# A two-layer hybrid encoder: how the low halves of its weights are made

## The chip, the cores and the metric

The kernel runs on one core of a Trainium2 chip. The metric is device time in microseconds (us); less is better. PE is TensorE (matrix multiply), ACT ScalarE, DVE VectorE, POOL GpSimd, and SP is SyncE, whose queue issues the DMAs (transfers between memories).

## The reference

Two layers of an encoder on 512 tokens of width 1024, each with three residual parts. The mixer runs four groups of attention heads side by side, gates and sums them. Then come cross-attention into 256 memory tokens and a squared-ReLU MLP of width 4096.

```python
for layer in range(DEPTH):                      # DEPTH = 2
    h = rms(x, g_mix[layer])
    (aq, ..., gate) = jnp.split(h @ w_in[layer], split_points, axis=-1)   # 1024 x 7584
    o_a = diff_attention(...)                   # 4 heads
    o_b = mla(...)                              # 8 heads, latent projections
    o_c = window_gqa(...)                       # 8 heads, window of 128
    o_d = axial_gqa(...)                        # 8 heads, rotary
    br = jnp.einsum('bsmc,mcd->bsmd', o, w_branch[layer])
    x = x + jnp.einsum('bsmd,bsmd->bsd', sigmoid(gate), br) @ w_out[layer]
    x = x + memory_xattn(rms(x, g_x[layer]), rms(mem, g_mem[layer]), ...)
    u = rms(x, g_mlp[layer]) @ w_up[layer]
    x = x + jnp.square(jax.nn.relu(u)) @ w_down[layer]
```

All inputs are float32. The large weights are read once per layer, from HBM.

## The kernel before, in words

Every product of two float32 matrices is made of three PE matmuls on float32r operands (`mm3`): each operand x is split into a high part hi (x rounded to float32r) and a low part lo = x - hi, and the sum hi·hi + hi·lo + lo·hi is accumulated. So each weight chunk needs a high and a low tile before PE can use it.

The weights are packed into 352 chunks of up to 128 x 1024 floats (512 KB). `wload` (line 292) handles one chunk: SP loads it into a raw tile `wst` (line 295), ACT casts it into the high tile `whi` (line 299), and POOL subtracts in four quarters, raw minus high, into the low tile `wlo` (line 302; in the profile it is the helper's line 167). There are two `wst` tiles, four `whi` and four `wlo` (line 121). A raw tile is free for its next load when its cast and its four subtractions are done; a high or low tile is free when PE has finished the matmuls that read it. `chain("w")` and `chain("wh")` keep loads and casts in the order of the program.

The work of one layer is in three stages. The mixer (0 to about 690 us in layer 0, 1205 to 1857 in layer 1) has twelve attention units; each unit's input projection takes four chunks, or one for the latent heads, and the gate and branch products (`gate_piece`, `branch_piece`) are put between attention steps as filling work, in the places that the string `FILL` gives. Then come the output projection and the cross-attention (690 to 862, 1857 to 2033), and the MLP (862 to 1205, 2033 to 2362): 32 chunks up and 32 down, one chunk per 24 matmuls of 512 columns, nothing else on PE. In the MLP each `up` piece also puts two ACT instructions (ReLU on the PSUM tile, then Square, lines 1121 and 1122), and every second one a low-part subtraction on POOL (line 1125).

POOL's other work is small: powers of -0.5 for the norms (`rpow`, lines 311 and 312, and similar ones), on 128 x 4 to 128 x 12 numbers. They stand in the same queue as the subtractions, and an engine takes its queue in order.

The order of instructions on each engine is set at build time by a scheduler that simulates the program; the kernel states only the program order and the chains.

Of the kernel before, what the change touches and what calls it, by code (L numbers as in the profile page):

```python
# [12 lines left out]
AF = mybir.ActivationFunctionType  # L13
ALU = mybir.AluOpType
# [79 lines left out]
def kernel(  # L94
# [18 lines left out]
    V, A, G, T, SY = nc.vector, nc.scalar, nc.gpsimd, nc.tensor, nc.sync  # L113
# [12 lines left out]
    def tl(tag, shape, dt=F32):  # L126
        cnt[0] += 1
        return sp.tile(shape, dt, tag=tag, name=f"{tag}{cnt[0]}", bufs=BUFS[tag])
# [26 lines left out]
    def f(ap):  # L155
        return ap.bitcast(F32)
# [9 lines left out]
    def sub_lo(dst, src, hi, eng=None):  # L166
        (eng or V).tensor_tensor(out=dst, in0=src, in1=f(hi), op=ALU.subtract)  # L167
# [16 lines left out]
    def chain(key, first, last=None):  # L184

        if key in tails:
            tc.add_manual_dep(first.ins, tails[key].name,
                              mybir.DependencyInfo(mybir.DependencyClass.NoSync, mybir.DependencyReason.DATA), reason=key)
        tails[key] = (last or first).ins
# [102 lines left out]
    def wload(key, tag="wst"):  # L292
        off, n = PLAN[key]
        st = tl(tag, [P, 1024])
        i = SY.dma_start(st[:, :n], bass.AP(tensor=wts.tensor, offset=wts.offset + off, ap=[[n, P], [1, n]]))
        chain("w", i)
        hi = tl("whi", [P, 1024], F32R)
        lo = tl("wlo", [P, 1024], F32R)
        chain("wh", A.copy(hi[:, :n], st[:, :n]))  # L299
        step = n // 4 if n % 4 == 0 else n // 2  # L300
        for c in range(0, n, step):
            sub_lo(lo[:, c:c + step], st[:, c:c + step], hi[:, c:c + step], G)
        return hi[:, :n], lo[:, :n]

    def wview(w, k):
# [124 lines left out]

    def front_A(l, norm, h):
        views = [wview(wload((l, "A", h, c)), k=2) for c in range(4)]
        vt = tl("v", [P, NTB, 2, P], F32R)
        Tq = tslot()
# [97 lines left out]

    def front_G(l, norm, br, g):
        views = [wview(wload((l, br, g, c)), k=2) for c in range(4)]
        vt = tl("v", [P, NTB, 3, 64], F32R)
        Tq = [tslot(), tslot()]
# [117 lines left out]

    def front_B0(l, norm, pre):
        views = [wview(w, k=2) for w in pre + [wload((l, "B", 0, c)) for c in range(len(pre), 4)]]
        cT = [slot(), slot(), slot()]
        toks = []
# [337 lines left out]
    for m in range(KD):  # L996
        SY.dma_start(X[m // 2][:, m % 2, :], xT[m * P:(m + 1) * P, :])
        if m % 2 == 0:
            c = m // 2
# [279 lines left out]
```

## Time and profile before

| | us |
|---|---|
| median of 3 runs | 2372.52 (2371.97 to 2377.07) |
| profiled execution, whole time | 2373.54 |
| its span, first to last instruction | 2371.8 |
| PE busy in the span | 2287.5 |
| POOL busy, all of it | 1304.7 |
| POOL busy with the weights' subtractions (1400 recorded) | 1079.1 |
| ACT busy with the weights' casts (350 recorded) | 349.9 |
| ACT busy, all of it | 1154.2 |

Between the span and the whole time lie 1.7 us. The granted clock of TensorE was 0.992 of full speed over the span. Matmuls overlap in the record: one of 512 columns shows 0.39 us, and the next starts 0.23 us after it. The busy share of an engine is a mean over stages; where the chain of waits names POOL or a DMA, PE was not the engine whose work ended last. Each wait is put down to one releaser, the one that came last.

### The profile page before, as it was taken

The numbers are of one execution on the slowest core, as the hardware profiler recorded it, in microseconds if no ns is written. First come the engines' busy times: TensorE is split into PE (matmuls) and PEld (weight loads), VectorE is DVE, ScalarE is ACT, GpSimd is POOL, SyncE is SP. The second block draws the span as 40 slices with busy tenths as digits, with TensorE's granted clock in tenths as the row PEclk, the third lists the DMA queues.
The fourth block names the chain that finished last, engine by engine and source line by source line (L and its number), as shares of the span: only waits on it lengthen the run. The fifth ranks groups of instructions, "written<-read, shape, count | busy, mean of one in ns | idle before, by whom it ended". The sixth has DMA issues, their size and how long they took to land.

```text
span 2371.8 us, 33721 instructions
## 1 busy us (share of the span) xinstructions
PE 2287.5 (96%) x12032; PEld 1963.8 (83%) x12032; DVE 1395.6 (59%) x2996; ACT 1154.2 (49%) x2269; POOL 1304.7 (55%) x1657
## 2 busy tenths in 40 slices
PE   7999999998999999999999999999999999999999
PEld 6788888887877788888888888898888778888887
DVE  6777676788964742222457676768888558322222
ACT  4555656655643642223345565566556446322321
POOL 7553454635365576666665435455453655766663
PEclk9999999999999999999999999999999999999999
DMA  5332242442454233333342213324425532323332
GB/s 169 103 96 68 89 138 76 138 145 80 151 170 151 76 98 96 91 98 98 107 132 92 87 56 106 133 78 150 131 88 168 169 107 85 103 94 98 98 93 85
DMA packets 90953, 260.36 MB, mean 110 GB/s; under 512 B 9832, under 2 KB 14568, under 8 KB 90784
## 3 DMA queue, kind: packets, MB, share of 16 engines
q1 hardware_dynamic: 90784, 258.20, 34.2%
q8 instruction: 95, 1.56, 0.3%
q14 instruction: 74, 0.61, 0.1%
HBM read 224.56 MB, written 33.60 MB: 109 GB/s over the span
## 4 chain that ended last, share of the span: by engine, by line
PE 73%; DVE 10%; POOL 7%; DMA 4%; ACT 3%; issue 3%; SPq 0%; POOLq 0%; ACTq 0%; DVEq 0%
PE dn L177 12%; PE dn L178 12%; PE dn L179 12%; PE df L177 9%; PE df L179 8%; PE df L178 8%; POOL wlo L167 5%; DMA wst<-in_wts_dram 3%; PE tr L476 2%; PE dn L403 1%; ACT whi L299 1%; DVE pt L480 1%; PE sc L177 1%; PE sc L178 1%; PE sc L179 1%
## 5 line engine op out<-in xcount | busy, mean ns | idle before, releaser
L167 POOL TENSOR_TENSOR wlo<-wst,whi 128x256 fp32r<-128x256 f32 (+3 forms) x1400 | 1079.1, 803 | 796.3 <-ACT whi L299 705.8
L299 ACT CAST whi<-wst 128x1024 fp32r<-128x1024 f32 (+3 forms) x350 | 349.9, 1002 | 663.3 <-PE dn L178 293.9
L177 PE MATMUL df<-s,whi 128*128 128x512 f32 (+1 forms) x967 | 383.2, 396 | 21.3 <-DVE zg L785 11.6
L178 PE MATMUL df<-s,whi 128*128 128x512 f32 (+1 forms) x967 | 376.7, 390 | 0.3 <-DVE s L167 0.3
L179 PE MATMUL df<-s,wlo 128*128 128x512 f32 (+1 forms) x967 | 376.8, 390 | 0.0
L177 PE MATMUL dn<-whi,s 128*128 128x384 f32 (+4 forms) x736 | 249.3, 345 | 12.0 <-ACT s L348 7.5
L178 PE MATMUL dn<-wlo,s 128*128 128x384 f32 (+4 forms) x736 | 250.0, 342 | 1.0 <-POOL wlo L167 1.0
L179 PE MATMUL dn<-whi,s 128*128 128x384 f32 (+4 forms) x736 | 250.1, 341 | 0.0
L177 PEld LDWEIGHTS df<-s,whi 128*128 128x128 f32 x967 | 182.8, 189 | 60.0 <-DVE zg L785 13.6
L179 PEld LDWEIGHTS df<-s,wlo 128*128 128x128 f32 x967 | 182.8, 189 | 37.1 <-POOL wlo L167 0.7
L178 PEld LDWEIGHTS df<-s,whi 128*128 128x128 f32 x967 | 182.9, 189 | 33.4 <-DVE s L167 0.8
L178 PE MATMUL dn<-s,whi 128*128 128x512 f32 (+1 forms) x529 | 198.8, 377 | 0.2 <-DVE s L167 0.2
L177 PE MATMUL dn<-s,whi 128*128 128x512 f32 (+1 forms) x529 | 198.0, 377 | 1.1 <-DVE s L976 0.9
L179 PE MATMUL dn<-s,wlo 128*128 128x512 f32 (+1 forms) x529 | 197.6, 374 | 0.0
L177 PEld LDWEIGHTS dn<-whi,s 128*128 128x128 f32 x736 | 140.1, 191 | 21.2 <-ACT s L348 7.5
L479 ACT CAST pt<-tr 128x512 fp32r<-128x512 f32 (+1 forms) x224 | 123.1, 557 | 68.6 <-PE tr L476 67.0
L480 DVE TENSOR_TENSOR pt<-tr,pt 128x512 fp32r<-128x512 f32 (+1 forms) x224 | 142.7, 643 | 20.0 <-ACT pt L479 9.5
L178 PEld LDWEIGHTS dn<-wlo,s 128*128 128x128 f32 x736 | 140.8, 191 | 11.0 <-POOL wlo L167 4.3
L179 PEld LDWEIGHTS dn<-whi,s 128*128 128x128 f32 x736 | 140.4, 191 | 5.3
L311 POOL TENSOR_SCALAR sf<-sf 128x8 f32<-128x8 f32 (+2 forms) x44 | 13.2, 299 | 193.7 <-DVE sf L415 192.0
L177 PEld LDWEIGHTS dn<-s,whi 128*128 128x128 f32 x529 | 99.7, 190 | 19.8 <-DVE s L976 1.1
L178 PEld LDWEIGHTS dn<-s,whi 128*128 128x128 f32 x529 | 100.4, 190 | 18.6 <-DVE s L167 0.6
(392 smaller groups left out, 4895.9 us busy)
## 6 DMA issues: line engine op xcount, KB each, us to landing
wst<-in_wts_dram SPq DMA_DIRECT2D x272, 512.0 KB, 3.6
wst<-in_wts_dram SPq DMA_DIRECT2D x64, 384.0 KB, 3.1
yl<-yz SPq DMA_DIRECT2D x48, 512.0 KB, 3.8
yz<-zg SPq DMA_DIRECT2D x64, 256.0 KB, 2.1
yz<-yl SPq DMA_DIRECT2D x48, 256.0 KB, 2.9
bias<-tscr SPq DMA_DIRECT2D x16, 320.0 KB, 3.5
yl<-yz SPq DMA_DIRECT2D x16, 256.0 KB, 3.1
bias<-tscr SPq DMA_DIRECT2D x8, 448.0 KB, 3.5
```

The lines of the kernel that those rows point to most:

```text
L167: (eng or V).tensor_tensor(out=dst, in0=src, in1=f(hi), op=ALU.subtract)
L177: a = T.matmul(ps, lhsT=lh, rhs=rh, start=first, stop=False)
L178: T.matmul(ps, lhsT=lh, rhs=rl, start=False, stop=False)
L179: b = T.matmul(ps, lhsT=ll, rhs=rh, start=False, stop=last)
L299: chain("wh", A.copy(hi[:, :n], st[:, :n]))
L311: G.tensor_scalar(dst, src, add, None, op0=ALU.add)
L403: T.transpose(ps[:rows_, i * P:(i + 1) * P], s, idn)
L476: T.transpose(ps[:, kb * P:(kb + 1) * P], src[:, kb * P:(kb + 1) * P], idn)
L479: A.copy(hi, pv)
L480: V.tensor_tensor(out=lo, in0=pv, in1=f(hi), op=ALU.subtract)
```

## The change

The four subtractions on POOL are replaced by two steps: ACT writes the negated high part into the low tile, and a DMA issued from POOL's queue adds the raw chunk onto it, element by element, in place.

```diff
         hi = tl("whi", [P, 1024], F32R)
         lo = tl("wlo", [P, 1024], F32R)
         chain("wh", A.copy(hi[:, :n], st[:, :n]))
-        step = n // 4 if n % 4 == 0 else n // 2
-        for c in range(0, n, step):
-            sub_lo(lo[:, c:c + step], st[:, c:c + step], hi[:, c:c + step], G)
+        A.activation(lo[:, :n], hi[:, :n], AF.Copy, scale=-1.0)
+        G.dma_start(out=f(lo[:, :n]), in_=st[:, :n], accum_op=ALU.add)
         return hi[:, :n], lo[:, :n]
```

Lines after 302 carry a number one less in the changed kernel. ACT gains one instruction per chunk. In the MLP of layer 0 its queue read before:

```order
922 L299 CAST whi_10667<-wst_10665 128x1024
923 L299 CAST whi_10704<-wst_10702 128x1024
924 L1121 ACTIVATE p_10582<-dn_10557 128x512
925 L1122 ACTIVATE p_10582<-p_10582 128x512
926 L299 CAST whi_10744<-wst_10742 128x1024
927 L299 CAST whi_10781<-wst_10779 128x1024
928 L1121 ACTIVATE p_10659<-df_10634 128x512
929 L1122 ACTIVATE p_10659<-p_10659 128x512
```

and at the same place it reads now (line 300 is the negation; `df` and `dn` are PSUM tiles that PE writes):

```order
1079 L299 CAST whi_10446<-wst_10444 128x1024
1080 L300 ACTIVATE wlo_10447<-whi_10446 128x1024
1081 L299 CAST whi_10481<-wst_10479 128x1024
1082 L1120 ACTIVATE p_10365<-df_10340 128x512
1083 L300 ACTIVATE wlo_10482<-whi_10481 128x1024
1084 L1121 ACTIVATE p_10365<-p_10365 128x512
1085 L299 CAST whi_10519<-wst_10517 128x1024
1086 L300 ACTIVATE wlo_10520<-whi_10519 128x1024
1087 L299 CAST whi_10554<-wst_10552 128x1024
```

The negation of every second chunk stands behind a ReLU that waits for PE.

POOL's queue in layer 0's mixer, at the second pair of powers of a projection (`sf` are norm sums), read before:

```order
81 L311 TENSOR_SCALAR sf_2720<-sf_2720 128x8
82 L312 TENSOR_TENSOR sf_2720<-sf_2720,mhalf 128x8
83 L167 TENSOR_TENSOR wlo_2883<-wst_2880,whi_2882 128x256 x4
84 L167 TENSOR_TENSOR wlo_3088<-wst_3085,whi_3087 128x256 x4
85 L311 TENSOR_SCALAR sf_2782<-sf_2782 128x8
86 L312 TENSOR_TENSOR sf_2782<-sf_2782,mhalf 128x8
87 L167 TENSOR_TENSOR wlo_3131<-wst_3128,whi_3130 128x192 x4
```

and now, with line 301 the accumulating DMA:

```order
79 L310 TENSOR_SCALAR sf_2658<-sf_2658 128x8
80 L311 TENSOR_TENSOR sf_2658<-sf_2658,mhalf 128x8
81 L301 DMA wlo_2821<-wst_2818 128x1024
82 L301 DMA wlo_3024<-wst_3021 128x1024
83 L310 TENSOR_SCALAR sf_2720<-sf_2720 128x8
84 L311 TENSOR_TENSOR sf_2720<-sf_2720,mhalf 128x8
85 L301 DMA wlo_3065<-wst_3062 128x768
```

The powers keep their places; between the two pairs stand two DMA issues where eight subtractions stood. The order of PE's instructions in both MLPs is the same in the two kernels (runs of 1506 and 1469 rows); in the mixers it differs in details.

## Rows read from the trace of the kernel before

**Rows 1.** The page's head, busy times, and shares of the chain that ended last.
```profile
span 2371.8 us, 33721 instructions
...
PE 2287.5 (96%) x12032; PEld 1963.8 (83%) x12032; DVE 1395.6 (59%) x2996; ACT 1154.2 (49%) x2269; POOL 1304.7 (55%) x1657
...
PE 73%; DVE 10%; POOL 7%; DMA 4%; ACT 3%; issue 3%; SPq 0%; POOLq 0%; ACTq 0%; DVEq 0%
```

**Rows 2.** Windows: stretch, us, busy us (instructions) by engine, clock, DMA, GB/s.
```profile
862.00:1205.00 343.00, 343.00 (x1502) 281.17 (x1501) 95.01 (x127) 107.21 (x136) 222.03 (x263) 1.00 0.34 101
690.00:862.00 172.00, 165.22 (x881) 138.06 (x880) 104.27 (x172) 85.58 (x163) 98.02 (x120) 0.99 0.39 119
0.00:690.00 690.00, 650.16 (x3693) 574.40 (x3694) 521.82 (x1232) 399.00 (x859) 352.11 (x473) 0.99 0.36 117
```

**Rows 3.** The chain of waits by line, 862 to 1205 us.
```profile
by line: PE dn L178 22.1%; PE dn L179 22.1%; PE dn L177 22.0%; PE df L177 11.2%; PE df L178 11.2%; PE df L179 11.2%; PE tr L364 0.2%
```

**Rows 4.** Timeline of ACT: start, us, engine, line, [idle before, releaser].
```profile
1002.38 1.05 ACT L299 CAST whi<-wst 128x1024 fp32r<-128x1024 f32 x1 [4.41 <-PE df L178]
1003.34 0.59 ACT L1121 ACTIVATE p<-df 128x512 f32<-128x512 f32 x1
1003.96 0.63 ACT L1122 ACTIVATE p<-p 128x512 f32<-128x512 f32 x1
...
1018.92 1.05 ACT L299 CAST whi<-wst 128x1024 fp32r<-128x1024 f32 x1 [3.33 <-PE df L178]
```

**Rows 5.** Timeline of POOL, same stretch.
```profile
1003.51 3.47 POOL L167 TENSOR_TENSOR wlo<-wst,whi 128x256 fp32r<-128x256 f32 x4 [2.30 <-ACT whi L299]
```

**Rows 6.** Waits of PE: releaser, us in total, times, longest.
```profile
PE dn L178 <- POOL wlo L167: 1.0, 3, 0.4
```

**Rows 7.** Chain of waits in time, 778 to 804 us: start, us.
```profile
782.07 3.54 DMA wst<-in_wts_dram
...
790.47 3.77 DMA wst<-in_wts_dram
...
795.44 3.92 POOL wlo L167 x4
...
799.38 3.62 DMA wst<-in_wts_dram
```

**Rows 8.** DMA issues: count, KB each, median us to landing.
```profile
wst<-in_wts_dram SPq DMA_DIRECT2D x272, 512.0 KB, 3.6
...
s<-in_xT_dram SPq DMA_DIRECT2D x8, 256.0 KB, 5.3
```

**Rows 9.** DMA queue, 862 to 1205 us: packets, MB, share.
```profile
q1 hardware_dynamic: 10160, 34.48, 33.3%
```

**Rows 10.** The chain of waits by line, the four stages outside the MLPs.
```profile
by line: PE df L177 8.6%; PE df L179 8.0%; PE df L178 8.0%; POOL wlo L167 6.7%; PE dn L177 5.8%; PE dn L178 5.7%; PE dn L179 5.5%; issue 4.9%; PE tr L476 4.0%; DMA wst<-in_wts_dram 3.7%; DVE zr L584 2.0%; DVE pt L480 2.0%; PE dn L403 1.8%; 
...
by line: POOL wlo L167 12.6%; PE dn L178 12.5%; PE dn L177 12.4%; PE dn L179 12.0%; DMA wst<-in_wts_dram 6.4%; PE df L177 5.0%; PE df L179 5.0%; PE df L178 5.0%; ACT whi L299 2.5%; PE sc L177 2.2%; PE sc L178 2.1%; PE sc L179 2.1%; PE tr L1
...
by line: PE df L177 8.2%; PE df L179 7.7%; PE df L178 7.7%; PE dn L177 6.4%; PE dn L179 6.3%; PE dn L178 6.2%; issue 4.8%; POOL wlo L167 4.7%; DMA wst<-in_wts_dram 4.1%; PE tr L476 3.4%; PE dn L403 2.2%; DVE pt L480 1.9%; ACT whi L299 1.7%;
...
by line: PE dn L177 13.6%; PE dn L178 13.6%; PE dn L179 13.2%; POOL wlo L167 9.1%; DMA wst<-in_wts_dram 8.2%; PE df L178 5.1%; PE df L179 4.8%; PE df L177 4.8%; ACT whi L299 2.3%; PE sc L177 2.3%; PE sc L178 2.2%; PE sc L179 2.2%; PE tr L17
```

**Rows 11.** Timeline of POOL in layer 0's mixer, around 288 us.
```profile
280.81 0.24 POOL L311 TENSOR_SCALAR sf<-sf 128x8 f32<-128x8 f32 x1 [5.22 <-DVE sf L415]
...
288.08 5.07 POOL L167 TENSOR_TENSOR wlo<-wst,whi 128x256 fp32r<-128x256 f32 x8 [5.27 <-ACT whi L299]
293.24 0.24 POOL L311 TENSOR_SCALAR sf<-sf 128x8 f32<-128x8 f32 x1
```

**Rows 12.** Timeline of DVE: one add beside POOL's subtractions, one without.
```profile
752.82 1.24 DVE L339 TENSOR_TENSOR of<-of,p 128x512 f32<-128x512 f32 x1
...
1915.41 0.68 DVE L339 TENSOR_TENSOR of<-of,p 128x512 f32<-128x512 f32 x1
```

**Rows 13.** Windows of line 299 alone: ACT busy us (casts).
```profile
0.00:690.00 690.00, 87.58 (x92) 0.99 0.36 117
```


## The prediction

> **What bounds the kernel now.** I read the page's head first: PE is busy 2287.5 of 2371.8 us, and the chain that ended last is 73% PE, 10% DVE, 7% POOL, 4% DMA, 3% ACT [rows 1]. Then the windows by stage: in the MLP PE is busy all of 343 us at full clock, in the mixer 650 of 690, in output projection and cross-attention 165 of 172 [rows 2]. So a gain can only come from outside the MLPs, and little of it.
>
> The MLP's chain of waits is PE alone [rows 3]. The reader is to see how the weights arrive there: ACT's casts come 5.51 us apart (1002.38 to 1018.92, three steps), each released by PE giving back a high tile [rows 4], and POOL's four subtractions end 3.47 us after they start, then POOL idles [rows 5]. That is a supply running four chunks ahead, held back by PE. PE waited for a low tile 1.0 us in the whole program [rows 6].
>
> In the other four stages the chain of waits contains the supply itself: POOL's `wlo`, the loads of `wst` and the casts, as far as the lines show them, are 10.4% of 690, 21.5% of 172, 10.5% of 652 and 19.6% of 176 us, together 212 us [rows 10]. In order of time it is a loop through one raw tile: load 3.54, cast 1.06, subtraction 3.4, load 3.77, cast, subtraction 3.92, load [rows 7]. The loads start 8.40 and 8.91 us apart, mean 8.66; about 0.25 of it is neither load (3.65), cast (1.06) nor subtraction (3.7).
>
> **The change, part by part.** *Removed*: 1400 subtractions on POOL. In the MLP they were hidden by PE, so there this is worth nothing. *Added on ACT*: one negation per chunk. ACT has no such row; the nearest is the cast of the same 128x1024 tile, 1.05 us [rows 4]; I take 1.06. ACT's queue in the MLP sets a ReLU (0.59 us) between cast and negation of every second chunk. *Added on POOL's queue*: one accumulating DMA per chunk, which waits for the negation; the raw tile is now free only when it has landed. *Moved*: nothing in PE's order in the MLPs.
>
> The price that decides is X, the time from the issue of the accumulating DMA to its landing. No transfer of this kind is in the trace. From below: a plain 512 KB load lands after 3.6 us [rows 8]; nothing suggests that reading, adding and writing back takes less. From above: the slowest landing in these rows, 5.3 us for 256 KB with many transfers in flight [rows 8], plus another 3.6 for the second operand, 8.9. In between: the 512 KB loads of the MLP keep 33.3% of the 16 DMA engines busy [rows 9], so one load costs 0.333 x 5.51 = 1.83 us of all of them; the second operand adds that once more, and as a third of the time a load is under way I add a third of it again, 0.6: 3.6 + 1.8 + 0.6 = 6.0. I take 6.0, nearer to the plain load than to the queue of the first microseconds.
>
> The loop through one raw tile then is 3.65 + 1.06 + 1.06 + 6.0 + 0.25 = 12.0 us instead of 8.66, and with two raw tiles one chunk comes per 6.0 us; in the MLP the ReLU makes it 12.6, one chunk per 6.3 us.
>
> - MLPs: PE wants a chunk every 5.51 us and gets one every 6.3. The four high tiles hide the first four of 128 chunks: 124 x 0.79 = +98 us. The cover goes where the loop passes 2 x 5.51 = 11.0, at X = 4.4.
> - Other stages, supply already on the chain: 212 x (12.0 / 8.66 - 1) = +82 us.
> - Other stages, supply not on the chain now: output projection and cross-attention take 24 chunks per layer, largely at the MLP's pace: 48 x (6.0 - 5.5) = +24 us. In the mixer 92 casts fall in 690 us, 7.5 us each [rows 2, 13], so the mean is covered, and I add nothing.
> - ACT: behind each negation stand the attention's exponentials and PSUM copies. ACT was 399 of 690 us busy in the mixer [rows 2], and 3% of the chain [rows 1]. Some 220 negations fall outside the MLPs; if one in fifteen delays the chain by its 1.06 us, +15 us; the bounds are 0 and, at one in four, 58.
> - POOL's queue: at 280.81 us a pair of powers runs, the next pair runs at 293.24, behind 5.07 us of subtractions [rows 11]. Now two DMA issues stand there, which wait for casts and negations. With an issue of some 1 us (bounds: 0, and the 2.5 us of one chunk's subtractions here) about 1.5 us is saved in each of some 16 such places, eight projections in halves per layer: -25 us.
> - DVE: an add of 128x512 takes 1.24 us beside the subtractions and 0.68 without [rows 12]. If an eighth of the chain's DVE time (10%, 237 us) is such stretching, -30 us. The two savings together I bound by -20 and -110.
>
> The Trainium skill's page SBUF — State Buffer, section "SBUF: two separate sides", agrees with the DVE row and adds what speaks against the change: a DMA of POOL's queue has its descriptors written by GpSimd, which is locked out while DVE runs an op in a two-port mode. No run here shows it yet; it would lengthen X where DVE is busiest, in the mixer.
>
> Sum: 98 + 82 + 24 + 15 - 25 - 30 = +164 us. Against the profiled execution's own 2373.5 (span 2371.8 and 1.7 around it) that gives 2538; this execution lies 1.0 above the median of the runs shown, so I forecast **2537 us**.
>
> **The rivals.**
>
> *1. The accumulating DMA lands like a plain load, and POOL's relief wins (faster).* With X = 3.6 the loop is 9.6 us: the MLPs lose nothing (10.2 / 2 = 5.1), the stages outside lose 212 x 0.11 = 23, ACT 15, and 55 is saved: -17, 2356 us. It decides as soon as the savings exceed 38 us. For it: 1079 us of POOL's work goes, and the waits of rows 11. Against it: PE waited for low tiles 1.0 us, and the new path has a step more. Here the Trainium skill's page DMA: Bandwidth & Descriptors, section "Anatomy of one DMA — SWDGE (gpsimd) path", gives a fit, 2.0 us plus bytes over 436e3; for 512 KB that is, as an estimate by that page, 3.2 us, and the sum by it 2346. The fit is one for copies, and the plain loads of this trace took 3.6, not 3.2.
>
> *2. Just covered.* X between 4.2 and 5: at 4.4 the loop is 10.4, the MLP exactly even, the rest +43 + 15 - 55 = +3, 2376 us; at 5, MLP +36, rest +57 + 15 - 55, 2426.
>
> *3. The DMA engines or their adder become the bound.* If the accumulate costs the engines three passes (two reads and a write, one after the other), a chunk takes 1.83 + 3 x 1.83 = 7.3 us of all 16, more than PE's 5.51; a long X comes to the same. At X = 8 the loop gives MLP 7.3 per chunk, +222, outside +131 and +72, ACT and savings -40: 2758. At 8.9: +278, +153, +94, -40, 2858. For it: engines already a third busy; against: nothing yet, the operation is not in the trace.
>
> *4. The change doesn't take load off POOL*, if generating a DMA holds it as long as the subtractions did, 3.5 us. Then savings vanish and X grows by that time; it ends in rival 3.
>
> **How the numbers follow.** Forecast, X from 5 to 8: 0.45, own range 2426 to 2758. Rival 2, X from 4.4 to 5: 0.13, slower by up to 53 us. Rival 3 with 4: 0.24. X under 4.4: 0.18, of which 0.14 is rival 1 (faster) and 0.04 ends within 0.2%, which is about 5 us and what a measurement of this kernel can tell from no change; I add 0.01 to that from rival 2. So faster 0.14, same 0.05, slower 0.81. The range goes from 2356 (X at its lower bound; half of rival 1 lies below) to 2870 (just past the upper bound, some 0.12 beyond): 0.81 inside.
>
> **What would show it.** In the changed profile: in the MLP windows PE no longer busy all the time, and the casts released by the loads instead of PE; their distance is the loop over two, 6.3 us expected. The chain of waits in the MLP should name the DMA `wlo<-wst`, and the DMA view its landing, 6.0. DMA share in the MLP from a third to about two thirds, near full in rival 3. L339-like DVE rows at 0.7 us everywhere would show the relief. Forecast wrong: casts still 5.5 us apart and released by PE (X under 4.4), or distances above 7.3.

## The result and the profile after

The changed kernel takes 2693.31 us (median of 4 runs, 2685.90 to 2716.57), the kernel before 2372.24 us beside it: a ratio of 1.1365, 95% interval 1.1291 to 1.1439. The forecast was 2537 us, slower by 6.9%; it went to 13.6%, inside the range of 2356 to 2870. The profiled execution took 2716.57 us, the longest of the four, with a span of 2714.8, 343.0 more than the span of before; the stages below add up to these 343, where the medians differ by 321. One run further below, 2738.82 us, lies more than 1.5% above the fastest of its kernel and enters no comparison.

The page's head, against [rows 1]:

```profile
span 2714.8 us, 33387 instructions
...
PE 2408.1 (89%) x12032; PEld 2011.8 (74%) x12032; DVE 1266.4 (47%) x2996; ACT 1460.9 (54%) x2621; POOL 532.4 (20%) x601
...
DMA 45%; PE 32%; issue 11%; ACT 8%; DVE 2%; POOL 1%; SPq 0%; POOLq 0%; ACTq 0%; DVEq 0%
DMA wlo<-wst 25%; DMA wst<-in_wts_dram 18%; PE dn L178 4%; PE dn L179 4%; PE df L177 4%; PE df L179 4%; PE dn L177 4%; PE df L178 4%; ACT wlo L300 3%; ACT whi L299 2%; PE tr L475 2%; PE sc L177 1%; PE sc L178 1%; PE sc L179 1%; DMA yl<-yz 1
```

The chain was 73% PE and 4% DMA; now it is 45% DMA, and 25% of the span is the accumulating DMA alone. POOL was relieved (1304.7 to 532.4 us busy), DVE too (1395.6 to 1266.4), and neither decides anything. PE works 120.6 us longer on the same 12032 matmuls, and the windows show why. They follow the stages of the changed kernel (stretch, us, busy us of PE, its weight loads, DVE, ACT, POOL, then clock, DMA share, GB/s), against [rows 2]:

```profile
0.00:833.00 833.00, 728.75 (x3893) 630.24 (x3894) 490.10 (x1262) 492.90 (x975) 172.62 (x204) 0.95 0.63 161
833.00:977.00 144.00, 120.17 (x655) 100.96 (x654) 66.89 (x136) 83.34 (x155) 21.16 (x27) 0.94 0.58 141
977.00:1391.00 414.00, 371.52 (x1504) 284.28 (x1503) 88.24 (x127) 169.07 (x205) 79.77 (x82) 0.98 0.72 164
```

In the MLP of layer 0 PE is idle 42 of 414 us where it was never idle, and the DMA share has gone from 0.34 to 0.72. In the mixer PE is idle 104 of 833 us, and its clock is 0.95 of full speed, so its work takes longer too; before, the mixer cut at the same place reads

```profile
0.00:735.00 735.00, 695.16 (x3890) 611.33 (x3891) 542.95 (x1261) 412.16 (x876) 375.38 (x501) 0.99 0.38 121
```

with 40 us idle. Two waits of PE and one of ACT in mixer 0 (releaser, us in total, times, longest):

```profile
PE dn L178 <- DMA wlo<-wst: 26.2, 11, 6.5
PE df L179 <- DMA wlo<-wst: 15.6, 10, 5.5
...
ACT whi L299 <- DMA wst<-in_wts_dram: 136.5, 40, 7.0
```

PE waits 41.8 us for low parts themselves, where it was 0.4 us before. ACT's casts wait 136.5 us for loads (41.1 before), and the attention's instructions stand behind them in ACT's queue.

Cut at the starts of the first addition of the output projection (line 1075 of before), of the MLP's first ReLU (line 1121) and of its last addition (line 1139), the profiled executions divide so:

| us | mixer 0 | projection, cross-attention 0 | MLP 0 | mixer 1 | projection, cross-attention 1 | MLP 1 |
|---|---|---|---|---|---|---|
| before | 735.1 | 116.3 | 345.3 | 710.2 | 115.3 | 345.5 |
| after | 832.9 | 143.7 | 414.5 | 789.5 | 138.7 | 391.7 |
| difference | +97.8 | +27.4 | +69.2 | +79.3 | +23.4 | +46.2 |

So the mixers pay 177 us, the MLPs 115 and the middle stages 51, together 343. (The middle stages are shorter here than in [rows 2], since part of their chunks is cut off to the mixer.)

The chain of waits in time, layer 0's MLP (start, us, what), answers [rows 3, 7]:

```profile
1198.45 4.36 DMA wst<-in_wts_dram
...
1202.89 0.04 ACT whi L299
...
1203.84 0.59 ACT p L1120
1204.43 0.95 ACT wlo L300
1205.39 0.28 issue
1205.67 6.91 DMA wlo<-wst
...
1212.63 4.55 DMA wst<-in_wts_dram
...
1220.05 6.22 DMA wlo<-wst
...
1226.32 4.13 DMA wst<-in_wts_dram
```

This is the forecast's loop, in its order: load, cast, ReLU, negation, accumulation, next load into the same raw tile. It runs 14.18 and 13.69 us, 6.97 per chunk with two raw tiles, where PE wants one every 5.51. (Over the whole stage it is less: 5.51 x 414.5 / 345.3 = 6.6 us per chunk, and 6.2 in layer 1.) The DMA view of 977 to 1391 us gives the price (queue, packets, MB, share of 16 engines; then issues, count, KB each, median us to landing), against [rows 8, 9]:

```profile
q0 software_dynamic: 9128, 33.12, 41.6%
q1 hardware_dynamic: 9912, 34.36, 30.6%
...
wlo<-wst POOLq DMA_DIRECT2D x62, 512.0 KB, 6.1
wst<-in_wts_dram SPq DMA_DIRECT2D x60, 512.0 KB, 4.2
```

X is 6.1 us here, 6.0 was taken. What the sum did not have is that the loads beside it became slower, from 3.6 to 4.2. In layer 1's MLP the two raw tiles fell into step for some 100 us, and the chain reads:

```profile
2401.17 5.24 DMA wlo<-wst
...
2406.47 3.73 DMA wst<-in_wts_dram
...
2412.71 4.42 DMA wlo<-wst
...
2417.18 4.61 DMA wst<-in_wts_dram
...
2424.31 4.45 DMA wlo<-wst
```

POOL now issues two accumulations 2.4 to 2.8 us apart, where it issued them some 7 us apart in the stretch above. So they run mostly beside each other, one lands after 4.4 to 5.2 us, and the loop is 11.54 and 11.60 us, 5.8 per chunk. It does not last. The issues of 2400 to 2500 us, and of 2500 to 2600:

```profile
wlo<-wst POOLq DMA_DIRECT2D x18, 512.0 KB, 4.8
...
wlo<-wst POOLq DMA_DIRECT2D x14, 512.0 KB, 6.3
```

PE is busy 99.7 of the first 100 us and 87.4 of the second. MLP 0 has both landings too: 6.7 us from 1060 to 1140, 4.8 from 1300 to 1373. So MLP 1's smaller loss (46 us against 69) fits more time in step, but no run holds the step fixed.

Two smaller answers, in the views by line (durations as minimum, median and maximum in ns). POOL's issue of the DMA in mixer 0, against [rows 5]:

```profile
L301 POOL DMA_DIRECT2D wlo<-wst x97: 850/863/1004, 7.7 to 832.4; - x97
```

And DVE's addition, now line 338, in 833 to 977 us, against [rows 12]:

```profile
L338 DVE TENSOR_TENSOR of<-of,p x21: 411/419/686, 841.5 to 965.1; 128x256 f32<-128x256 f32 x14, 128x512 f32<-128x512 f32 x7
```

An issue holds POOL 0.86 us instead of 3.47 for the subtractions (rival 4 wanted 3.5), and none of these additions takes 1.24 us any more.

Last, what such a wait leaves behind on PE. In mixer 0 the chain names an accumulation from 264.94 to 270.61 us and a load from 270.66 to 273.65; the windows around them:

```profile
265.00:268.00 3.00, 1.10 (x7) 0.71 (x6) 1.97 (x4) 2.06 (x6) 1.10 (x3) 1.00 1.04 205
...
274.00:277.00 3.00, 1.27 (x8) 0.68 (x7) 1.95 (x4) 2.95 (x7) 1.19 (x2) 1.00 0.63 122
...
278.00:281.50 3.50, 3.50 (x17) 2.75 (x15) 0.73 (x2) 0.65 (x2) 0.00 (x0) 0.57 1.03 216
281.50:285.00 3.50, 3.50 (x21) 3.22 (x20) 1.89 (x4) 2.73 (x5) 0.41 (x1) 1.00 0.78 261
```

PE works 1.10 of the first 3 us, is busy from 268 to 274, works 1.27 of the next 3 us and is busy again from 277; then the granted clock falls to 0.57 for 3.5 us (most of it at 1.2 instead of 2.4 GHz) before it is full again. So a wait can be paid twice: once idle, once at the lower clock.

### The profile page after: what moved, and what is told of

It is laid out like the page before. It is cut to its first block, busy times and chain, and to the rows that moved or that the text cites. A ratio compares the mean times of both kernels' runs of the same rounds, so it can differ in the third digit from the quotient of the medians.

```text
span 2714.8 us, 33387 instructions
## 1 busy us (share of the span) xinstructions
PE 2408.1 (89%) x12032; PEld 2011.8 (74%) x12032; DVE 1266.4 (47%) x2996; ACT 1460.9 (54%) x2621; POOL 532.4 (20%) x601
## 3 DMA queue, kind: packets, MB, share of 16 engines
q0 software_dynamic: 50688, 173.82, 34.2%
## 4 chain that ended last, share of the span: by engine, by line
DMA 45%; PE 32%; issue 11%; ACT 8%; DVE 2%; POOL 1%; SPq 0%; POOLq 0%; ACTq 0%; DVEq 0%
DMA wlo<-wst 25%; DMA wst<-in_wts_dram 18%; PE dn L178 4%; PE dn L179 4%; PE df L177 4%; PE df L179 4%; PE dn L177 4%; PE df L178 4%; ACT wlo L300 3%; ACT whi L299 2%; PE tr L475 2%; PE sc L177 1%; PE sc L178 1%; PE sc L179 1%; DMA yl<-yz 1%
## 5 line engine op out<-in xcount | busy, mean ns | idle before, releaser
L301 POOL DMA_DIRECT2D wlo<-wst x350 | 309.1, 883 | 1731.9 <-ACT wlo L300 1452.2
L179 PE MATMUL df<-s,wlo 128*128 128x512 f32 (+1 forms) x967 | 394.4, 408 | 45.8 <-DMA wlo<-wst 45.4
L177 PE MATMUL df<-s,whi 128*128 128x512 f32 (+1 forms) x967 | 396.7, 410 | 37.3 <-DVE yl L806 16.5
L178 PE MATMUL df<-s,whi 128*128 128x512 f32 (+1 forms) x967 | 388.7, 402 | 0.0
L300 ACT ACTIVATE wlo<-whi 128x1024 fp32r<-128x1024 f32 (+3 forms) x352 | 354.1, 1007 | 4.6
L178 PE MATMUL dn<-wlo,s 128*128 128x384 f32 (+4 forms) x736 | 262.5, 357 | 57.7 <-DMA wlo<-wst 57.5
L177 PE MATMUL dn<-whi,s 128*128 128x384 f32 (+4 forms) x736 | 255.3, 352 | 14.1 <-ACT s L347 8.1
L179 PE MATMUL dn<-whi,s 128*128 128x384 f32 (+4 forms) x736 | 257.8, 350 | 0.0
L177 PEld LDWEIGHTS df<-s,whi 128*128 128x128 f32 x967 | 191.0, 197 | 80.9 <-DVE yl L806 20.5
L178 PEld LDWEIGHTS df<-s,whi 128*128 128x128 f32 x967 | 191.2, 198 | 36.1 <-DVE s L167 0.4
L177 PEld LDWEIGHTS dn<-whi,s 128*128 128x128 f32 x736 | 144.2, 196 | 24.9 <-ACT s L347 8.1
L179 PEld LDWEIGHTS dn<-whi,s 128*128 128x128 f32 x736 | 145.6, 198 | 5.4
L179 PEld LDWEIGHTS dn<-s,wlo 128*128 128x128 f32 x529 | 102.7, 194 | 60.5 <-DMA wlo<-wst 43.1
L177 PEld LDWEIGHTS dn<-s,whi 128*128 128x128 f32 x529 | 101.6, 193 | 39.4 <-ACT p L1120 10.0
```

The source lines that it names most:

```text
L177: a = T.matmul(ps, lhsT=lh, rhs=rh, start=first, stop=False)
L178: T.matmul(ps, lhsT=lh, rhs=rl, start=False, stop=False)
L179: b = T.matmul(ps, lhsT=ll, rhs=rh, start=False, stop=last)
L300: A.activation(lo[:, :n], hi[:, :n], AF.Copy, scale=-1.0)
L301: G.dma_start(out=f(lo[:, :n]), in_=st[:, :n], accum_op=ALU.add)
```

## The experiments

The first theory (A) was the forecast's: the loop through one raw tile. Against it stood ACT's work (B) and the DMA engines as a hard bound (C); later came the lateness of the low part itself (A2, then L), the traffic on the DMA engines (D, then T) and the order of the queues, whatever a transfer costs (E). Stages are given in the order of the table above, from the profiled execution. The scheduler orders each of these kernels anew. Only the plain copy below has the changed kernel's order on PE, ACT and DVE; in the mixers of the others the order differs, and a difference between two mixers holds that too.

**The DMA left out.**

```diff
         A.activation(lo[:, :n], hi[:, :n], AF.Copy, scale=-1.0)
-        G.dma_start(out=f(lo[:, :n]), in_=st[:, :n], accum_op=ALU.add)
```

> The changed kernel without the accumulating DMA: the low tile holds only the negated high part, so the products with it are not the reference's. ACT's work is that of the changed kernel, POOL has no weight work, the raw tile is free after the cast. Theory A (two raw tiles held through load, cast, negation and accumulating DMA supply the weights too late, and that is the whole loss): about 2340 us, from 2373 less the savings of 55 plus 15 for ACT, MLPs at 345 us each. Theory B (ACT's negations delay the attention in the mixers, whose two stages lost 177 us): 2480 us or more, mixers still above 780 us. Theory C (the DMA engines' total work): as A here.

2339.12 us (2336.51 to 2341.57), ratio 0.9863 (0.9849 to 0.9878). Stages 719.9, 113.5, 343.8, 701.2, 113.8, 343.8. Mixer 0:

```profile
0.00:720.00 720.00, 692.19 (x3892) 612.79 (x3893) 487.67 (x1262) 490.50 (x975) 86.30 (x105) 0.98 0.38 124
```

ACT's time for the negations is not what makes the kernel slower (B falls as the main cause): with all of them, and no work for the weights on POOL, it is 32 us faster than before. With the accumulating DMA it is 354 us slower than this.

**ACT's negation with POOL's addition.**

```diff
-        G.dma_start(out=f(lo[:, :n]), in_=st[:, :n], accum_op=ALU.add)
+        step = n // 4 if n % 4 == 0 else n // 2
+        for c in range(0, n, step):
+            G.tensor_tensor(out=lo[:, c:c + step], in0=st[:, c:c + step], in1=f(lo[:, c:c + step]), op=ALU.add)
```

> ACT negates as in the changed kernel, but POOL adds the raw chunk in four quarters instead of the DMA: the negation alone, no new transfer. Theory A: the loop through a raw tile grows from 8.66 by one negation, 1.1 us, to 9.8; 212 us of supply on the chain grow by 13%, 28 us, and 15 for ACT: 2415 us, MLPs unchanged at 345 us. Theory B: 2500 us or more.

2424.66 us, ratio 1.0224 (1.0208 to 1.0239). Stages 754.4, 116.9, 346.6, 737.5, 116.8, 346.6. The added step costs 53 us over before when POOL still does the sum, nearly all of it in the mixers. The way from chunk to low part is 1.06 us longer, and ACT's queue is fuller; the two are not parted here.

**The second operand from HBM,** so that the raw tile is free after the cast.

```diff
-        G.dma_start(out=f(lo[:, :n]), in_=st[:, :n], accum_op=ALU.add)
+        G.dma_start(out=lo[:, :n], in_=bass.AP(tensor=wts.tensor, offset=wts.offset + off, ap=[[n, P], [1, n]]),
+                    accum_op=ALU.add)
```

> The accumulating DMA takes the chunk from HBM again instead of from the raw tile, which is then free after its cast. As many accumulating transfers, more HBM reads. Theory A: the loop through a raw tile falls to load and cast, about 5.4 us or 2.7 per chunk; the low tiles (four) have time; MLPs back at 345 us, total 2370 to 2430 us. Theory C (16 DMA engines loaded with some 5 us of work per chunk): MLPs stay above 390 us, total above 2600.

2566.82 us, ratio 1.0834 (1.0791 to 1.0878): neither number. The stages say more: 810.6, 137.3, 343.8, 786.0, 132.0, 343.8. Windows of its MLP and its mixer:

```profile
948.00:1291.00 343.00, 343.00 (x1493) 280.25 (x1492) 81.38 (x126) 168.20 (x205) 78.48 (x81) 1.00 0.89 196
0.00:811.00 811.00, 720.15 (x3914) 625.92 (x3915) 488.63 (x1262) 491.37 (x975) 173.16 (x204) 0.96 0.66 168
```

The MLP is back at PE's pace, with the DMA engines 0.89 busy. So the raw-tile loop was the MLP's whole loss (A), and the engines are no bound there (C falls). But of the mixers' 177 us, 151 remain without the loop, though ACT's casts in mixer 0 now wait only 8.6 us for loads. (In mixer 0 an accumulation lands after 7.4 us here, 5.2 in the changed kernel, so the loop's own share may be more than the 26 that went.)

**A third raw tile,** with smaller pools of small tiles to make room.

```diff
-    BUFS = dict(s=14, T=6, wst=2, whi=4, wlo=4, tok=4, spl=2, v=2, bias=2, p=5, z=1, zr=1, zg=2, yl=2, of=1, pt=3, st=24,
-                sf=8)
+    BUFS = dict(s=14, T=6, wst=3, whi=4, wlo=4, tok=4, spl=2, v=2, bias=2, p=4, z=1, zr=1, zg=2, yl=2, of=1, pt=3, st=18,
+                sf=4)
```

> The changed kernel with three raw tiles instead of two; to make room p has 4 buffers instead of 5, st 18 instead of 24, sf 4 instead of 8. Theory A: the loop of 13.9 us gives a chunk per 4.6 us, below PE's 5.5: MLPs back at about 345 us, mixers lose at most half of what they lost, total 2380 to 2460 us. Theory C: more transfers in flight only stretch each other, MLPs above 390 us, total above 2600.

2551.04 us, ratio 1.0762 (1.0742 to 1.0781); stages 820.6, 132.9, 342.9, 771.5, 130.6, 344.4. Its MLP:

```profile
954.00:1296.00 342.00, 342.00 (x1491) 279.09 (x1490) 80.90 (x125) 168.16 (x204) 77.69 (x80) 1.00 0.87 197
```

The same answer by another road: the MLPs whole, the mixers still 147 us over before.

**The smaller pools alone,** with two raw tiles (`wst=2`, p, st and sf as above).

> The changed kernel with the smaller pools of the run with three raw tiles (p 4, st 18, sf 4), but two raw tiles: what the smaller pools cost. 2690 to 2720 us; if it is above 2750, the run with three raw tiles gained more than it showed.

2692.60 us, one run; the changed kernel's four took 2685.90 to 2716.57. So no cost of the smaller pools shows, and what the third tile gave (142 us) is not theirs.

**Only the first eighth accumulated.**

```diff
-        G.dma_start(out=f(lo[:, :n]), in_=st[:, :n], accum_op=ALU.add)
+        G.dma_start(out=f(lo[:, :n // 8]), in_=st[:, :n // 8], accum_op=ALU.add)
```

> The changed kernel with an accumulating DMA over the first eighth of each chunk only; the rest of the low tile stays the negated high part, so the output is not the reference's. Same instructions, queues and waits, an eighth of the bytes. Theory A2 (what the mixers lose is the latency of the low part: after each projection the four tiles refill, and the first matmul on a chunk waits cast, negation and X) and theory D (the bytes load the DMA engines and delay the other transfers) both expect about 2340 to 2390 us, X near 2.5 us. Theory E (waits and order on POOL's and ACT's queues, whatever the transfer costs): 2500 us or more.

2413.91 us, ratio 1.0175 (1.0158 to 1.0192), some 24 us above what A2 and D expected and far below E. Stages 747.2, 122.3, 346.1, 727.1, 120.7, 346.6. Window of mixer 0:

```profile
0.00:747.00 747.00, 698.73 (x3890) 611.46 (x3891) 488.42 (x1261) 492.46 (x975) 176.96 (x204) 0.98 0.45 126
```

and its DMA issues:

```profile
wlo<-wst POOLq DMA_DIRECT2D x59, 64.0 KB, 2.4
```

A DMA that lands 2.4 us after its issue already costs the mixers 27 and 26 us against the run without the DMA, with the DMA share at 0.45 (0.38 there).

**Traffic that nobody waits for:** no accumulation, but per chunk two plain DMAs into HBM tiles that are never read.

```diff
-        G.dma_start(out=f(lo[:, :n]), in_=st[:, :n], accum_op=ALU.add)
+        for src, w in ((hi, n), (lo, 3 * n // 4)):
+            cnt[0] += 1
+            G.dma_start(out=dp.tile([P, 1024], F32, tag="nul", name=f"nul{cnt[0]}", bufs=8)[:, :w], in_=f(src[:, :w]))
```

> As the run with the negation alone (2339 us; the low tile is the negated high part, not the reference's), plus two plain DMAs per chunk on POOL's queue that copy 1.75 chunks' bytes from the high and low tile to a place in HBM that nothing reads: about the accumulating DMAs' load on the 16 engines, but nobody waits for a low part. Theory A2: 2340 to 2375 us. Theory D: mixers at 780 us or more each, total 2450 us or more.

2399.45 us, ratio 1.0114 (1.0098 to 1.0130): between the two. Stages 755.6, 113.9, 343.8, 724.5, 114.2, 343.8.

```profile
0.00:756.00 756.00, 710.34 (x3915) 622.89 (x3916) 489.92 (x1262) 491.00 (x975) 195.27 (x303) 0.97 0.65 226
```

At a DMA share of 0.65 (0.63 in the changed kernel) the mixers lose 36 and 23 us to the run without the DMA, and MLPs and middle stages nothing. The loads of mixer 0:

```profile
wst<-in_wts_dram SPq DMA_DIRECT2D x61, 512.0 KB, 6.1
```

They land after 6.1 us, against 3.8 without the DMA and 4.2 in the changed kernel. So this traffic delays them more than the accumulation does, and 36 and 23 us are rather too much for traffic than too little.

**A plain copy instead of the accumulation.**

```diff
-        G.dma_start(out=f(lo[:, :n]), in_=st[:, :n], accum_op=ALU.add)
+        G.dma_start(out=f(lo[:, :n]), in_=st[:, :n])
```

> The changed kernel with a plain copy in place of the accumulating DMA (the low tile becomes the raw chunk, so the output is not the reference's): same queue, bytes written and waits, without the second operand. If the second operand and the adder are what makes X long, X falls from 6.2 in the MLP to about 4.4, the loop to 12 us, a chunk per 6.0: total 2500 to 2570 us. If the queue's kind and the sharing make it long, 2650 us or more.

2431.27 us (2 runs), ratio 1.0252 (1.0224 to 1.0280), better than either expectation. Stages 762.7, 127.6, 343.9, 727.9, 122.5, 345.5. Its queue and landing:

```profile
q0 software_dynamic: 45568, 173.82, 17.9%
...
wlo<-wst POOLq DMA_DIRECT2D x272, 512.0 KB, 3.4
```

The changed kernel's, in the same view of the whole run:

```profile
q0 software_dynamic: 50688, 173.82, 34.2%
...
wlo<-wst POOLq DMA_DIRECT2D x272, 512.0 KB, 5.2
```

The copy's mixer 0:

```profile
0.00:763.00 763.00, 706.12 (x3893) 616.38 (x3894) 489.97 (x1262) 492.66 (x975) 142.04 (x204) 0.98 0.53 176
```

The same bytes land after 3.4 instead of 5.2 us, with 17.9% of the engines instead of 34.2%. The addition on the way costs 262 of the 321 us. This is the cleanest comparison of all: the rows of PE, ACT and DVE (12032, 2621 and 2996) come in the changed kernel's order. The mixers are 70 and 62 us shorter than there, the middle stages 16 each, and the MLPs are back at PE's pace; over before, the mixers still lose 28 and 18. What the run doesn't part is the landing and the load on the engines, which fall together. For such a copy the Trainium skill's page DMA: Bandwidth & Descriptors, section "Anatomy of one DMA — SWDGE (gpsimd) path", gives 3.2 us as an estimate by its fit; 3.4 agrees; the accumulation's 5.2 lies well above it.

**The low part late, with few bytes.**

```diff
-        G.dma_start(out=f(lo[:, :n]), in_=st[:, :n], accum_op=ALU.add)
+        for _ in range(3):
+            G.dma_start(out=f(lo[:, :n // 8]), in_=st[:, :n // 8], accum_op=ALU.add)
```

> The low part comes late, but few bytes move: three accumulating DMAs of the first eighth of the chunk, one after the other (each waits for the one before on the same numbers), in place of one over the whole chunk. The other seven eighths of the low part stay the negated high part, and the first eighth gets the raw part three times. The DMAs of 64 KB landed after 2.3 us each, so the low part should be complete some 7 us after the negation, as in the changed kernel or later, with a sixth to a quarter of the engine time of q0 instead of 34%. Theory L (lateness: the mixers' +177 us come from low parts that land 5 to 7 us after the negation): mixers about as long as in the changed kernel, 790 to 860 us each, total 2690 to 2850. Theory T (traffic: the mixers lose by the engines' time that the accumulation takes from other transfers): mixers within 25 us of those with one small DMA (747 and 727), while the MLPs still lose by the loop, (3.65 + 1.06 + 1.06 + 0.6 + 7.0 + 0.25) / 2 = 6.8 us per chunk, +80 us each: total 2570 to 2650.

3073.64 us, ratio 1.2976 (1.2921 to 1.3032), beyond both. Stages 913.1, 155.6, 476.4, 898.2, 155.4, 472.9. Mixer 0:

```profile
0.00:913.00 913.00, 756.23 (x3887) 645.04 (x3888) 493.10 (x1261) 494.86 (x973) 341.56 (x397) 0.92 0.46 115
```

One low part in the chain of waits:

```profile
298.05 2.27 DMA wlo<-wst
...
300.60 3.48 DMA wlo<-wst
...
304.60 2.23 DMA wlo<-wst
```

POOL's largest wait (us in total, times, longest):

```profile
POOL wlo L302 <- DMA wlo<-wst: 924.6, 517, 5.6
```

The DMA engines are hardly busier than with one small DMA (0.46 to 0.45), and the mixer is 166 us longer: traffic is not needed for the loss. But the test is not clean. POOL's queue itself waits for each DMA of a chunk (924.6 us), so the DMAs of different chunks hardly overlap, and one low part took 8.8 us (298.05 to 306.83). Another run followed.

**Late, with traffic, and POOL's queue free.**

```diff
-        G.dma_start(out=f(lo[:, :n]), in_=st[:, :n], accum_op=ALU.add)
+        for w in (n, n // 2):
+            cnt[0] += 1
+            G.dma_start(out=dp.tile([P, 1024], F32, tag="nul", name=f"nul{cnt[0]}", bufs=8)[:, :w], in_=f(hi[:, :w]))
+        G.dma_start(out=f(lo[:, :n // 8]), in_=st[:, :n // 8], accum_op=ALU.add)
```

> Lateness and traffic apart, with POOL's queue free: per chunk two plain DMAs from the high tile to HBM tiles that nobody reads (the whole chunk and half of it), and behind them in the same queue the accumulating DMA of the first eighth alone. The other seven eighths of the low part stay the negated high part. The traffic is that of the run with two plain copies that nobody waited for (mixers 756 and 725 us, MLPs 343.8 each, total 2399), but now the low part and the raw tile are held until the small DMA behind the copies has landed, some 5 to 6 us after the negation. Theory L (the mixers of the changed kernel lose mostly by the lateness): mixers 795 to 850 and 760 to 815 us, and the MLPs lose by the loop as in the changed kernel, 380 to 420 each: total 2580 to 2740. Theory T (by the traffic): mixers within 25 us of 756 and 725; with the MLPs' loss by the loop total 2470 to 2570.

2579.68 us, ratio 1.0890 (1.0872 to 1.0909). Stages 778.9, 134.0, 379.7, 759.4, 136.5, 379.7.

```profile
0.00:779.00 779.00, 704.70 (x3894) 610.56 (x3895) 489.85 (x1262) 490.50 (x973) 283.21 (x397) 0.98 0.64 207
```

and its issues of the small DMA:

```profile
wlo<-wst POOLq DMA_DIRECT2D x57, 64.0 KB, 4.1
```

In mixer 0 the small DMA landed 4.1 us after its issue; 5 to 6 after the negation had been expected. Against the run with two copies that nobody waited for, at the same DMA share, waiting for it costs the mixers 23 and 35 us, the middle stages 20 and 22, and the MLPs, by the loop, 36 each. In the mixers that is between the two theories: against the run without the DMA, traffic takes 36 and 23 us and lateness 23 and 35 more. This split is an estimate: the order differs between the runs, and the loads of mixer 0 land after 4.1 us here instead of 6.1, so lateness may hold more. Up to the changed kernel, 54 and 30 are left, where the landing is 5.2 us instead of 4.1 and the clock 0.95 instead of 0.98; of the 54, 24 are PE's longer work (728.75 against 704.70) and 30 are idle.

**Two ways to do better, from the kernel before.** A third raw tile there, with the pools as above:

> The kernel before with three raw tiles instead of two, room made by smaller pools of small tiles (p 4, st 18, sf 4), subtractions on POOL as before. Theory of the loop (outside the MLPs before is held by load, cast and subtraction through one raw tile, and the loads stand on the chain with some 78 us): a third tile takes the loads off the chain, 2300 to 2345 us. Rival (POOL's own 3.4 to 3.9 us per chunk is the pace there, and the loads only stand next to it; or the four high and low tiles are what runs out): 2360 to 2390 us.

2380.18 us, ratio 1.0040 (1.0025 to 1.0056); mixers 736.5 and 722.6. So a third tile with smaller pools gave nothing, although loads stood on the chain of before [rows 10]; what the smaller pools cost there no run shows. And the first of the four quarters on DVE:

```diff
-            sub_lo(lo[:, c:c + step], st[:, c:c + step], hi[:, c:c + step], G)
+            sub_lo(lo[:, c:c + step], st[:, c:c + step], hi[:, c:c + step], V if c == 0 else G)
```

> The kernel before with the first of the four quarter subtractions of each chunk on DVE instead of POOL. Theory R (what freed POOL gave, 32 us with no weight work there at all, is the time of the subtraction on the way to PE): a quarter less on POOL, 0.85 us per chunk, gives 8 to 25 us: 2347 to 2365 us. Rival S (DVE's queue is in order and full of attention work in the mixer, and DVE and POOL slow each other, an add took 1.24 instead of 0.68 us): the first quarter comes later than POOL would have made it, 2375 to 2420 us.

2378.60 us, ratio 1.0031 (1.0019 to 1.0044). The middle stages got 6.6 and 6.0 us shorter, the mixers 7.3 and 5.7 longer. The costliest groups (instructions | busy us, mean ns | idle before, releaser):

```profile
L167 POOL TENSOR_TENSOR wlo<-wst,whi 128x256 fp32r<-128x256 f32 (+3 forms) x1050 | 862.8, 849 | 960.4 <-ACT whi L299 906.9
L167 DVE TENSOR_TENSOR wlo<-wst,whi 128x256 fp32r<-128x256 f32 (+3 forms) x350 | 207.3, 592 | 294.5 <-ACT whi L299 293.7
```

A quarter took POOL 771 ns before (1079.1 us over 1400) and takes 849 now, so POOL sheds 216 us instead of 270, and DVE takes on 207 in return. No version that beats the kernel before was found.

## Why the prediction was right, and where not

The direction and the loop were foreseen. That the time lies inside the range is in part luck: the loss was 321 us where 165 were forecast, and by the sum a loss of 321 needs an X of about 7.4, while X was 5.2 over the run and 6.1 in the MLP. More than half of the loss came from the mixers, where the sum had next to nothing.

- **The loop through one raw tile, in the MLPs: right, shown.** Freeing the raw tile early or adding one takes the MLPs back to 343 to 344 us, two independent edits, and so does the copy with its shorter landing. The term was +98 us and measured +115. X was right (6.1 for 6.0), but the load beside it was 4.2 instead of 3.65, and the loop 13.9 instead of 12.6; by the sum's own way that is 124 x (6.97 - 5.51) = 181 us. That the term still came near is luck: for part of both stages the tiles fell into step at 5.8 per chunk, which the sum did not foresee.
- **The middle stages: near in size, in part by luck.** +24 and the part of the +82 that the chain's shares of 172 and 176 us carry (71.5 us of the 212, times 0.386, 28) make 52; measured +51, but over stages of 116 us here against 172 there. The cause is less sure: freeing the raw tile gave back only a quarter to somewhat over a third of it (137.3 and 132.0 from HBM, 132.9 and 130.6 with the third tile), and the run late behind copies lost 20 and 22 us more than the run with copies that nobody waited for.
- **ACT's +15 and the savings of 55: not contradicted, not shown apart.** Together -40; the run with the negation alone is 32 us faster than before, but there no low part is waited for at all. The run with POOL's addition (+53) shows that a negation on the way to the low part does cost. ACT's term priced each negation at its own 1.06 us; that casts in the same queue would wait for late loads, with the attention behind them, is in no term.
- **The failed step: the mixer, "so the mean is covered, and I add nothing".** With its share of the 82 (54 us), ACT and the savings, the forecast had the mixers at about +14 us; they lost 177. The mean of 7.5 us per chunk did not cover it: PE waited 41.8 us for low parts in mixer 0 alone. Four high and four low tiles are all the store there is; that this store is too small is argued, as no run had more of them. What is shown is that the loss hangs on the accumulating DMA: without it the mixers are faster than before, and with a copy that lands after 3.4 us, in the same order, 132 of the 177 us are gone. Inside that, the runs point to two causes, traffic (up to +36 and +23 us against the run without the DMA) and lateness of the low part (+23 and +35 more for a DMA that lands after 4.1 us). The clock adds to both. PE's busy time in mixer 0 rises by and large as it falls: 695.16 us at 0.99, 710.34 at 0.97, 720.15 at 0.96, 728.75 at 0.95, 756.23 at 0.92. From before to the changed kernel that is 34 of the 98 us. Freeing the raw tile changes the mixers by 26 to 30 of 177 us. How the last 54 and 30 us divide between the longer landing, the clock and the order of the instructions stays open; no run held two of them fixed.
- **Rival 1** needed X under 4.4, and X was 5.2 over the whole run. It would not have come true with a shorter one either: the copy landed after 3.4 us, where the sum gives some 2350, and took 2431, as the mixers still lost 28 and 18 us. **Rival 2** needed X under 5. **Rival 3** is rejected as a bound on the engines, since the MLP ran at PE's pace with a DMA share of 0.89. **Rival 4** fell with the issue of 0.86 us. The lock-out of descriptor writing that the Trainium skill's page SBUF — State Buffer, section "SBUF: two separate sides", names did not show between the stages: the issue takes 0.86 us and the landing 5.2 in the mixer, where DVE is busiest, and 0.88 and 6.1 in the MLP. The two stages differ in traffic too, so a small lock-out is not excluded.

## What to carry to other kernels

Before a step is moved from an engine to a DMA, compare the time from start to landing, not the engine's busy time: POOL's 3.5 us of work were replaced by 1 us on ACT and 5 to 6 in flight, while the tile they hold and the consumer both wait. Work the loop through the scarcest buffer at the duration of a transfer that runs beside the other transfers, and don't take a stage's mean demand as cover where only a few tiles stand between producer and consumer. Taking POOL's 1079 us away, with the negations on ACT in their place and nothing waiting for a low part, was worth 32 us here.

## What the runs showed of the hardware

- A DMA that accumulates 512 KB from SBUF into SBUF took 34.2% of the engines' span of 2714.8 us for 173.82 MB; as a plain copy the same bytes took 17.9% of 2434.0. That is 928 against 436 us, 2.1 times. The Trainium skill's page Collectives: The Full Stack, section "The bandwidth ceiling: the fold count and why AG ≠ RS ≠ AR", says for collectives that an addition on the way needs two source reads, and gives a measured ratio of 1.93 between the bandwidths without and with it. This case agrees with the direction and comes out a little higher, in engine time.
- The same accumulation landed after 4.4 to 5.2 us mostly beside another accumulation (2400 to 2430 us) and after 6.2 to 6.9 beside loads (1205 to 1226 us). Two tiles stayed in one pattern for some 100 us and then changed to the other.
- Issuing an accumulation held POOL 0.87 us, of 512 KB or of 64 KB alike, and issuing a copy of 512 KB 0.54 us (medians of 350 issues each).
- In the mixer of layer 0 the granted clock was 0.95 over the stage. From 278 to 281.5 us it was 0.57, after PE had worked 1.27 of the 3 us from 274.
